# The first layer's second feed-forward sweep as seven block products, block sums formed in place, and the last sweep's residual work spread over ten tiles

## The chip, the cores and the metric

The kernel runs on one core of one Trainium2 chip. The metric is the device time of one execution in microseconds (us), taken as the median of several runs. Every number ahead of the prediction comes from the kernel before the change.

## The reference

Two layers of a diffusion backbone run over 1024 latent tokens and 256 context tokens, with 1024 features. The first layer mixes tokens with a convolution module, the second with attention. Each is followed by a feed-forward part, and that part is what the change touches:

```python
def swiglu(h, w1, w3, w2):
    return (jax.nn.silu(h @ w1) * (h @ w3)) @ w2
...
x = x + gf_x * rmsnorm(swiglu(fx, ffn_w1[i], ffn_w3[i], ffn_w2[i]), norm_g[i, 3])
```

All data are float32. The inner width of the feed-forward part is 2816, that is 22 tiles of 128.

## The kernel before

**Numbers as pairs.** Each float32 operand is split into a high part, rounded to the multiply format (`wh`), and a rest (`wl`). ACT casts the high part, DVE subtracts to get the rest (`split`, L158; `wload`, L137, for a weight just loaded). A product of two operands then takes three matmuls per block of 128 inner values: high by high, high by rest, rest by high (`mm3`, L166).

**Sweeps.** Activations lie with features on partitions and tokens along the free axis. The tokens are worked in three pieces: C (256 context tokens), L (the first 512 latent tokens) and R (the last 512). The function `ffn` (L790) makes one sweep over the 22 inner tiles. Layer one has two sweeps: the first for C and L, the second for R. Layer two has two as well: the first for L, the second for R. For each inner tile, `up` loads a 128x1024 tile of `w1` and one of `w3`, splits them, makes 48 matmuls of 512 columns, and forms the hidden tile. The 22 tiles form six groups of 4, 4, 4, 4, 3 and 3. After the first tile of the next group, `down` multiplies a group's hidden tiles by `w2` (96 matmuls of 512 columns for four tiles), and adds the result into the sweep's output (`evict`, L912, whose addition is L917). The last group is finished by `last` (L937).

**Block products.** In layer two's second sweep, all tiles but the first use `up_fast` (L844): `w1` and `w3` of that tile are taken as a 2x2 block matrix, the activations too (halves of the features by halves of the tokens), and the four block results come out of seven products in place of eight. Each product is 12 matmuls of 256 columns, 84 for a tile. The sums of activation blocks are formed once, by `forms` (L768). The sums of weight blocks are formed by DVE for each tile, into a tile of their own (`sums`, in the buffer KB), and then split. The weights come through three raw buffers (`self.raws`: two named `wr`, one named `q`), taken in turn by `raw` (L98). The split weights go to `wh` and `wl`, three buffers each, also in turn.

**Order.** Each engine runs its own list of instructions from first to last. The lists are made when the program is built, by a scheduler that looks at the dependencies, so an engine can have work of several tiles interleaved. Background work (residuals and norms of the pieces already done, and a first part of the attention's projections) is written as generators in a queue `bgq`. `pump` (L123) draws from it a share of each feed-forward step: 0.5 us of work per us of matmuls. In layer one's second sweep that background is `early` (L1351): the residuals of C and L (`final`, rows L692 and L695), the norm of C, the projections of C, and the norm of L (`apply`, rows L398, L403 and L404). In layer two's second sweep it is the residual of L.

Of the kernel before, what the change touches and what calls it, by code (L numbers as in the profile page):

```python
# [55 lines left out]
class Kern:  # L56
# [710 lines left out]

    def forms(self, x, tags, box):  # L768
# [18 lines left out]
        yield
        box += [(f[:, i, 0], f[:, i, 1]) for f in fs for i in range(2)]

    def ffn(self, l, fs, ytags, htags, boxes, tanh=False, parts=1, tail=None, fast=None):  # L790
# [53 lines left out]
        def up_fast(ft):  # L844

            n = ns[0] // 2
            xh, xl = fs[0][0]
            fm, sums = fast
            B11, B21, B22 = [lambda k, r=r, c=c: (xh[:, 4 * r + k, c * n:(c + 1) * n], xl[:, 4 * r + k, c * n:(c + 1) * n])
                             for r, c in ((0, 0), (1, 0), (1, 1))]  # L850
            T1, T2, T3, T4 = [lambda k, f=f: (f[0][:, k, :], f[1][:, k, :]) for f in fm]
            r1, r3 = self.raw(), self.raw()
            nc.sync.dma_start(r1, self.a["w1"][l, ft])
# [9 lines left out]
            def prod(out, w, x, first=True):  # L863
                for k in range(4):
                    (wh, wl), (bh, bl) = w(k), x(k)
                    nc.tensor.matmul(out, lhsT=wh, rhs=bh, start=first and k == 0, stop=False, skip_group_check=not first)  # L866
                    nc.tensor.matmul(out, lhsT=wh, rhs=bl, start=False, stop=False, skip_group_check=not first)  # L867
                    nc.tensor.matmul(out, lhsT=wl, rhs=bh, start=False, stop=k == 3, skip_group_check=not first)  # L868
            X = self.bank("sx")[:, :n]
            Y, Z = self.bank("sy")[:, :n], self.bank("mm")[:, :n]  # L870
            sa, h = self.sm(2 * n), self.sm(2 * n)
# [6 lines left out]
            nc.vector.tensor_tensor(s2, s1, a11, op=ALU.subtract)  # L878
# [4 lines left out]
            nc.scalar.copy(sa[:, n:], X)  # L883
            s3, s4 = sums[:, 1, :512], sums[:, 1, 512:]
            nc.vector.tensor_tensor(s3, a11, a21, op=ALU.subtract)
            nc.vector.tensor_tensor(s4, a12, s2, op=ALU.subtract)
# [4 lines left out]
            nc.vector.tensor_tensor(h[:, n:], h[:, n:], X, op=ALU.add)  # L891
            A22, = two(a22, 512)
            prod(X, A22, T4, False)
            nc.vector.tensor_tensor(sa[:, n:], sa[:, n:], Y, op=ALU.add)
            nc.scalar.activation(sa, sa, AF.Silu)
            nc.vector.tensor_tensor(h[:, n:], sa[:, n:], h[:, n:], op=ALU.mult)
            nc.vector.tensor_tensor(h[:, :n], sa[:, :n], X, op=ALU.mult)
            i = ft % (GRP + 1)
# [84 lines left out]
    def qk_pair(self, psE, psO, n, g, rope, wk, highs, sink, rq=None):  # L983
# [6 lines left out]
        self.qk += 1  # L990
        EO = wk[:, o:o + 2, :n]
        t12 = highs[self.qk % len(highs)][:, :, :n]
        E, O, t1, t2 = EO[:, 0], EO[:, 1], t12[:, 0], t12[:, 1]
# [40 lines left out]
    def qkv(self, h, col0, n, wk, rope=None, highs=()):  # L1034
# [3 lines left out]
        lat0 = col0 - CTX  # L1038
        highs = [wk[:, 6:8], *highs]
        if rope is not None:  # L1040
# [134 lines left out]
    def build(self):  # L1175
# [159 lines left out]
        self.bgq.append(rest_R())  # L1335
        for us in self.ffn(0, [(fv["C"][0], CTX), (fv["L"][0], 512)], (room[:, :2048].rearrange("p (k n) -> p k n", k=KT), "T5"), ("KB", "HS"),
                           (zv["C"], zv["L"])):
            self.pump(0.5 * us)
        self.drain()

# [8 lines left out]
        hC, hL, hR = [], [], []  # L1349

        def early():  # L1351
            yield from final(0, zv["C"][0], self.x1d, self.x2d, *PIECES["C"], 0, "KB")
            yield from final(0, zv["L"][0], self.x1d, self.x2d, *PIECES["L"], 0, "KB")
# [3 lines left out]
            wk = self.T("KB", [P, 8, 256])  # L1357
            yield from self.qkv(hC[0], 0, CTX, wk)
            self.xv = [self.cp.tile([P, 4], F32, tag=f"xv{i}", name=f"xv{i}") for i in range(2)]
            yield from self.norm_in(1, None, (None, "T3", "T2"), CTX, CTX + 512, hL, xt=zv["L"][0][0], keep=self.xv[0])  # L1360
# [27 lines left out]
    def attention(self, final, qr):  # L1388
# [102 lines left out]
        for i, us in enumerate(self.ffn(1, [(fL[0], 512)], ("T4",), ("HS",), (zL,), tanh=True)):  # L1491
            self.pump(0.95 * us)
            if i >= FT + 4 * (len(GROUPS) - 1) - 1:
                if fg is None:
                    self.drain()
                    fg = self.forms(yR[2], ("T6", "T3"), fm)
                next(fg, None)
# [3 lines left out]
        out = a["out"]  # L1501
        sums = self.T("KB", [P, 2, 1024])
        self.raws.append(self.room())
# [59 lines left out]
        for i, us in enumerate(self.ffn(1, [(fR[0], 512)], ("T1",), ("HS",), (zR,), parts=2, tail=(first, second),  # L1563
                                        fast=(fm, sums))):
            self.pump(0.5 * us)
            if i == FT + 4 * (len(GROUPS) - 1) - 1:
# [112 lines left out]
```

## Time and profile before

| What | Value |
|---|---|
| Median of 3 runs | 2950.51 us (2949.70 to 2955.74) |
| The profiled execution's own time | 2950.76 us |
| Its span, first to last instruction | 2949.0 us |
| Mean granted TensorE clock | 0.987 |
| Layer one's first sweep ends, second begins | at 1072.9 us of the span |
| Layer one's second sweep | 1072.9 to 1453.9 us |
| Layer two's second sweep up to `last` | 2578.9 to 2915.4 us |
| DVE busy over the span | 2034.8 us (69%) |
| ACT busy over the span | 1274.2 us (43%) |

The profile has one row for a group of instructions: the line of the kernel, the engine, the operation, the tile written and the tiles read (`wl<-wr,wh` writes `wl` from `wr` and `wh`; `ps` is the matmul result memory), how many, and the mean duration of one in ns. Behind the last bar stands how long the engine stood idle just before them, and which instruction ended the wait. PE is the matrix engine; DVE, ACT and POOL are the vector, scalar and GpSimd engines, and SP starts DMAs.

### The profile page before, as it was taken

The page shows a single profiled execution, that of the slowest core. Times are in us where ns is not written, and L with a number is a line of the kernel's source. Part 1 is how long each engine was busy: PE and PEld are TensorE (multiplying, and loading weights), DVE is VectorE, ACT ScalarE, POOL GpSimd, SP SyncE. Part 2 cuts the span into 40 slices and gives each one's busy share as a digit, 9 for nine tenths or more (in the row PEclk, how much of TensorE's full clock was granted, in tenths as well). Part 3 has the DMA queues.
Part 4 walks back from the last instruction along what each step waited for, and adds up shares of the span by engine and source line. Part 5 has one row for each costly group of instructions (what it writes and reads, how often), then busy time and mean ns, then how long its engine had stood idle before and what let it go on. Part 6 is the DMA issues. An engine that isn't in the chain of part 4 may idle for free.

```text
span 2949.0 us, 40809 instructions
## 1 busy us (share of the span) xinstructions
PE 2866.7 (97%) x15706; PEld 2424.9 (82%) x15706; DVE 2034.8 (69%) x3524; ACT 1274.2 (43%) x2118; POOL 223.2 (8%) x377
## 2 busy tenths in 40 slices
PE   8999989999999999999999999989999999999998
PEld 6888877888888888888878787767777778889997
DVE  6887887847556368433586899786666666776777
ACT  5222255432222134222345688645555543444444
POOL 0000001011122010000011111110000000010000
PEclk9999999999999999999999999999999999999999
DMA  6443434334355234332345211322222143343332
GB/s 248 132 126 98 122 126 149 128 126 131 110 175 187 65 115 150 107 97 89 129 161 164 88 46 45 102 81 81 70 69 83 60 136 97 123 167 94 101 99 88
DMA packets 131459, 336.46 MB, mean 114 GB/s; under 512 B 31297, under 2 KB 52833, under 8 KB 130113
## 3 DMA queue, kind: packets, MB, share of 16 engines
q1 hardware_dynamic: 77728, 222.33, 23.6%
q0 software_dynamic: 29344, 103.83, 10.9%
q10 hardware_dynamic: 24192, 7.70, 1.1%
q8 instruction: 123, 2.02, 0.3%
q14 instruction: 72, 0.58, 0.1%
HBM read 289.50 MB, written 38.93 MB: 111 GB/s over the span
## 4 chain that ended last, share of the span: by engine, by line
PE 88%; DVE 7%; DMA 2%; issue 2%; ACT 1%; POOL 0%; ACTq 0%; SPq 0%; DVEq 0%; POOLq 0%
PE ps L172 17%; PE ps L173 17%; PE ps L174 17%; PE ps L1100 4%; PE ps L1118 4%; PE ps L866 2%; PE ps L1124 2%; PE ps L868 2%; PE ps L453 2%; PE ps L867 2%; PE ps L454 2%; PE ps L1125 2%; PE ps L455 2%; PE ps L184 2%; PE ps L185 2%; PE ps L183 2%
## 5 line engine op out<-in xcount | busy, mean ns | idle before, releaser
L172 PE MATMUL ps<-T,wh 128*128 128x512 f32 (+1 forms) x1696 | 636.8, 376 | 0.6 <-DVE sm L830 0.4
L174 PE MATMUL ps<-T,wl 128*128 128x512 f32 (+1 forms) x1696 | 633.9, 374 | 3.0 <-DVE wl L148 3.0
L173 PE MATMUL ps<-T,wh 128*128 128x512 f32 (+1 forms) x1648 | 615.0, 373 | 0.1
L144 ACT CAST wh<-wr 128x1024 fp32r<-128x1024 f32 (+1 forms) x259 | 269.4, 1040 | 573.9 <-PE ps L173 416.3
L148 DVE TENSOR_TENSOR wl<-wr,wh 128x1024 fp32r<-128x1024 f32 (+1 forms) x259 | 313.0, 1209 | 225.0 <-ACT wh L144 222.2
L174 PEld LDWEIGHTS ps<-T,wl 128*128 128x128 f32 x1696 | 321.6, 190 | 58.0 <-DVE wl L148 3.6
L172 PEld LDWEIGHTS ps<-T,wh 128*128 128x128 f32 x1696 | 321.7, 190 | 56.1 <-ACT T L1463 1.7
L173 PEld LDWEIGHTS ps<-T,wh 128*128 128x128 f32 x1648 | 312.5, 190 | 52.4 <-DVE T L164 1.4
L1122 DVE TENSOR_TENSOR T<-ps,T 128x512 fp32r<-128x512 f32 x320 | 216.9, 687 | 108.4 <-ACT T L1121 107.6
L1121 ACT CAST T<-ps 128x512 fp32r<-128x512 f32 x320 | 186.1, 586 | 191.0 <-PE ps L1118 177.2
L173 PE MATMUL ps<-HS,wh 128*128 128x512 f32 x656 | 257.7, 393 | 0.0
L172 PE MATMUL ps<-HS,wh 128*128 128x512 f32 x608 | 238.4, 392 | 0.0
L174 PE MATMUL ps<-HS,wl 128*128 128x512 f32 x608 | 237.7, 391 | 0.0
L1118 PE MATMUL ps<-cst,T 128*128 128x128 f32 x1100 | 189.5, 275 | 3.1 <-DVE T L1122 3.1
L1106 DVE TENSOR_SCALAR_CACHE_REDUCE T<-ps,rq 128x1280 f32<-128x1280 f32 x110 | 170.1, 1546 | 28.0 <-PE ps L1100 22.1
L1118 PEld LDWEIGHTS ps<-cst,T 128*128 128x128 f32 x1100 | 132.8, 141 | 49.4 <-DVE T L1122 30.2
L866 PE MATMUL ps<-T,wh 128*128 128x256 f32 x588 | 167.2, 285 | 2.4 <-ACT wh L161 2.4
L868 PE MATMUL ps<-T,wl 128*128 128x256 f32 x588 | 165.4, 282 | 3.5 <-DVE wl L164 3.5
L1108 ACT ACTIVATE T<-T,mn 128x1280 f32<-128x1280 f32 x110 | 150.5, 1368 | 38.6 <-DVE T L1106 38.2
L867 PE MATMUL ps<-T,wh 128*128 128x256 f32 x588 | 165.2, 281 | 0.0
L917 DVE TENSOR_TENSOR T<-ps,T 128x512 f32<-128x512 f32 (+1 forms) x168 | 110.6, 662 | 77.7 <-PE ps L174 73.3
L1100 PE MATMUL ps<-KB,q 128*128 128x512 f32 (+1 forms) x576 | 145.2, 370 | 5.3 <-DVE HS L1106 3.1
(340 smaller groups left out, 5704.5 us busy)
## 6 DMA issues: line engine op xcount, KB each, us to landing
wr<-in_w SPq DMA_DIRECT2D x200, 512.0 KB, 3.5
q<-in_w SPq DMA_DIRECT2D x40, 512.0 KB, 3.5
wr<-in_pw SPq DMA_DIRECT2D x35, 512.0 KB, 3.6
HR<-in_wmodT POOLq DMA_DIRECT2D x56, 256.0 KB, 3.9
q<-in_wmodT POOLq DMA_DIRECT2D x56, 256.0 KB, 3.9
q<-qsd POOLq DMA_DIRECT2D x32, 256.0 KB, 3.3
wr<-in_wo SPq DMA_DIRECT2D x16, 512.0 KB, 3.6
qsd<-T POOLq DMA_DIRECT2D x14, 512.0 KB, 4.8
```

The lines of the kernel that those rows point to most:

```text
L144: nc.scalar.copy(hi, raw)
L148: nc.vector.tensor_tensor(lo, raw, hi.bitcast(F32), op=ALU.subtract)
L172: nc.tensor.matmul(out[:, :n], lhsT=wh, rhs=xh, start=k == 0, stop=False)
L173: nc.tensor.matmul(out[:, :n], lhsT=wh, rhs=xl, start=False, stop=False)
L174: nc.tensor.matmul(out[:, :n], lhsT=wl, rhs=xh, start=False, stop=k == nk - 1)
L866: nc.tensor.matmul(out, lhsT=wh, rhs=bh, start=first and k == 0, stop=False, skip_group_check=not first)
L867: nc.tensor.matmul(out, lhsT=wh, rhs=bl, start=False, stop=False, skip_group_check=not first)
L868: nc.tensor.matmul(out, lhsT=wl, rhs=bh, start=False, stop=k == 3, skip_group_check=not first)
L1100: nc.tensor.matmul(sc[:, k0:k0 + w], lhsT=q[:, h, :], rhs=kt[:, p * TOK + k0:p * TOK + k0 + w], start=p == 0, stop=p == 1)
L1118: nc.tensor.transpose(tp[:, h * P:(h + 1) * P], Ps[h][:, j * P:(j + 1) * P], c["ident"])
L1121: nc.scalar.copy(ph, tp)
L1122: nc.vector.tensor_tensor(pl, tp, ph.bitcast(F32), op=ALU.subtract)
```

## The change

The activation forms for layer one's second sweep are now made too: four DVE additions rebuild the float32 activations of R from their pairs (`both` in `forms`), then the forms are made as in layer two. Six of the eight steps are placed between the last steps of the first sweep, two behind the first tile of the second. The sums of weight blocks are written over the raw weights, one of them into a small buffer named `sb`, so that the weights are split in another order: the two top blocks, one sum alone (512 wide), a sum with a bottom block, and two sums. KB is then free. In layer two it gives two more raw buffers, five in all; in layer one there are three as before. Layer one's background takes 0.2 us per us up to the last group. The main part of the norm of L moves into a generator `late`, run beside `last` at 2.0. Layer two's share goes from 0.5 to 0.1.

```diff
+    def forms(self, x, homes, box, both=None):
...
+        if both is not None:
+            for b, k, c in ((b12, 0, 1), (b11, 0, 0), (b22, 4, 1), (b21, 4, 0)):
+                hi, lo = (v[:, k:k + 4, c * n:(c + 1) * n].bitcast(F32) for v in both)
+                nc.vector.tensor_tensor(b, hi, lo, op=ALU.add)
+                yield
...
             A11, A12 = two(r1)
             prod(X, A11, B11)
             prod(Z, A12, B21)
             nc.scalar.copy(sa[:, :n], X)
-            s1, s2 = sums[:, 0, :512], sums[:, 0, 512:]
-            nc.vector.tensor_tensor(s1, a21, a22, op=ALU.add)
-            nc.vector.tensor_tensor(s2, s1, a11, op=ALU.subtract)
-            S1, S2 = two(sums[:, 0])
+            tt(a11, a11, a21, ALU.subtract)
+            tt(s2, a22, a11, ALU.subtract)
+            S2, = two(s2, 512)
             prod(X, S2, T2, False)
-            nc.vector.tensor_tensor(sa[:, :n], sa[:, :n], Z, op=ALU.add)
+            tt(sa[:, :n], sa[:, :n], Z, ALU.add)
+            tt(a21, a21, a22, ALU.add)
+            S1, A22 = two(r3)
             prod(Y, S1, T1)
             nc.scalar.copy(sa[:, n:], X)
-            s3, s4 = sums[:, 1, :512], sums[:, 1, 512:]
-            nc.vector.tensor_tensor(s3, a11, a21, op=ALU.subtract)
-            nc.vector.tensor_tensor(s4, a12, s2, op=ALU.subtract)
-            S3, S4 = two(sums[:, 1])
+            tt(a12, a12, s2, ALU.subtract)
+            S3, S4 = two(r1)
             prod(X, S3, T3, False)
             nc.scalar.copy(h[:, n:], Y)
             prod(Y, S4, B22, False)
...
-            A22, = two(a22, 512)
             prod(X, A22, T4, False)
...
+            yield from self.qkv(hC[0], 0, CTX, None)
+            for _ in range(KT):
+                yield next(gl)
+
+        def late():
+            yield from gl
             self.wk = self.T("T5", [P, 8, 512])
+        gl = self.norm_in(1, None, (None, "T3", "T2"), CTX, CTX + 512, hL, xt=zv["L"][0][0], keep=xv[0])
         self.raws.append(self.room())
-        self.set_banks(mm=[0, 1, 2, 3], st=[5, 6], cv=[4, 7])
+        self.set_banks(mm=[0, 1, 2], sx=[3, 4], sy=[7], st=[5, 6])
         self.bgq.append(early())
-        for us in self.ffn(0, [(fv["R"][0], 512)], ("T1",), ("HS",), (zv["R"],)):
-            self.pump(0.5 * us)
+        for i, us in enumerate(self.ffn(0, [(fv["R"][0], 512)], ("T1",), ("HS",), (zv["R"],), fast=fm)):
...
+            if i == FT + 4 * (len(GROUPS) - 1) - 1:
+                self.drain()
+                self.bgq.append(late())
+                self.set_banks(mm=[0, 1, 2, 3], st=[5, 6], cv=[4, 7])
+            self.pump((0.2 if i < FT + 4 * (len(GROUPS) - 1) else 2.0) * us)
...
-        sums = self.T("KB", [P, 2, 1024])
+        more = self.T("KB", [P, 2, 1024])
+        self.raws += [more[:, 0], more[:, 1]]
         self.raws.append(self.room())
...
-            self.pump(0.5 * us)
+            self.pump(0.1 * us)
```

What this does to the order is shown at three places.

**First place: a plain tile of layer one's second sweep, on DVE and ACT** (the 17th tile, number 16; its raw buffers are `wr_73` for `w1` and `wr_74` for `w3`). Before, a tile of the same sweep was this on DVE (L836 is the hidden tile's multiplication, L148 the rest of a loaded weight, L164 the rest of the hidden tile, `HS`):

```order
L836 TENSOR_TENSOR sm<-sm,ps 128x512
L148 TENSOR_TENSOR wl<-wr_74,wh 128x1024
L164 TENSOR_TENSOR HS<-sm,HS 128x512
L148 TENSOR_TENSOR wl<-q,wh 128x1024
```

Now DVE has this (all of `up_fast`'s sums are recorded at L879, all of its splits at L164; `sb` is the small sum, `sm` the halves of the result):

```order
L879 TENSOR_TENSOR wr_73<-wr_73,wr_74 128x512
L879 TENSOR_TENSOR sm<-sm 128x256
L879 TENSOR_TENSOR sm<-sm,ps 128x256
L879 TENSOR_TENSOR sb<-wr_74,wr_73 128x512
L879 TENSOR_TENSOR wr_74<-wr_74 128x512
L164 TENSOR_TENSOR HS<-sm,HS 128x512
L164 TENSOR_TENSOR wl<-sb,wh 128x512
L879 TENSOR_TENSOR sm<-sm,ps 128x256
L164 TENSOR_TENSOR wl<-wr_74,wh 128x1024
L879 TENSOR_TENSOR wr_73<-wr_73,sb 128x512
L164 TENSOR_TENSOR wl<-wr_73,wh 128x1024
```

And ACT has this beside it (L885, L894 and L898 copy results out of `ps`: after the first, the third and the fourth product; L903 is the silu):

```order
L903 ACTIVATE sm<-sm 128x512
L161 CAST HS<-sm 128x512
L161 CAST wh<-sb 128x512
L885 COPY sm<-ps 128x256
L161 CAST wh<-wr_74 128x1024
L894 COPY sm<-ps 128x256
L161 CAST wh<-wr_73 128x1024
L898 COPY sm<-ps 128x256
```

The third row on DVE reads the last product of tile 15, and the sum `sb` for tile 16 now stands behind it; the sum into `wr_73`, whose split feeds the fifth product, stands behind the split of the two blocks in `wr_74`. On ACT the cast of that last pair stands behind the copy L894, which waits for the third product. Four tiles have the cast of `sb` ahead of the silu's hidden tile but the same last rows; the tile behind each `down` has all its casts ahead of L894.

**Second place: a plain tile of layer two's second sweep, on ACT.** Before (L875, L883 and L889 are the copies out of `ps`, L895 the silu):

```order
L875 COPY sm<-ps 128x256
L161 CAST HS<-sm 128x512
L161 CAST wh<-wr_73 128x512
L883 COPY sm<-ps 128x256
L161 CAST wh<-wr_74 128x1024
L889 COPY sm<-ps 128x256
L161 CAST wh<-KB 128x1024
L895 ACTIVATE sm<-sm 128x512
```

Now:

```order
L161 CAST wh<-sb 128x512
L903 ACTIVATE sm<-sm 128x512
L161 CAST wh<-KB 128x1024
L161 CAST HS<-sm 128x512
L885 COPY sm<-ps 128x256
L161 CAST wh<-wr_74 128x1024
L161 CAST wh<-KB 128x1024
L894 COPY sm<-ps 128x256
L898 COPY sm<-ps 128x256
```

The copy after the third product (L883 before, L894 now) moved behind two more 1024-wide casts: the tile's last pair and the next tile's first pair. In the first group of this sweep three tiles still have the last pair's cast behind it.

**Third place: the end of layer one's second sweep, on DVE, while `last` runs on PE.** Before (L917 adds a result from `ps` into the output, L390 sums squares, `q`, `wr_73` and `wr_74` are weights):

```order
L164 TENSOR_TENSOR HS<-sm,HS 128x512
L917 TENSOR_TENSOR T_8784<-ps,T_8784 128x512 x2
L390 TENSOR_TENSOR acc<-acc,sb 128x512
L917 TENSOR_TENSOR T_8784<-ps,T_8784 128x512
L148 TENSOR_TENSOR wl<-q,wh 128x1024
L390 TENSOR_TENSOR acc<-acc,sb 128x512
L917 TENSOR_TENSOR T_8784<-ps,T_8784 128x512
```

Now (L925 is the addition that was L917; L398 and L404 make the norm of L):

```order
L164 TENSOR_TENSOR HS<-sm,HS 128x512
L925 TENSOR_TENSOR T_8800<-ps,T_8800 128x512 x2
L148 TENSOR_TENSOR wl<-q,wh 128x1024
L390 TENSOR_TENSOR acc<-acc,sb 128x512
L398 SCALAR_TENSOR_TENSOR sb<-T_4324,col_7900,ps 128x512 x3
L404 SCALAR_TENSOR_TENSOR T_12381<-sb,mod_103,T_12380 128x512 x3
L398 SCALAR_TENSOR_TENSOR sb<-T_4324,col_7900,ps 128x512 x3
L404 SCALAR_TENSOR_TENSOR T_12381<-sb,mod_103,T_12380 128x512 x3
L925 TENSOR_TENSOR T_8800<-ps,T_8800 128x512 x2
```

Twelve instructions of the norm of L now stand between the second and the third addition of `last`'s results. `last` has eight results and four banks of `ps` for them.

More of the change, by code (lines that the diff above doesn't have):

```diff
@@ L847, in up_fast @@
             xh, xl = fs[0][0]
-            fm, sums = fast
             B11, B21, B22 = [lambda k, r=r, c=c: (xh[:, 4 * r + k, c * n:(c + 1) * n], xl[:, 4 * r + k, c * n:(c + 1) * n])
                              for r, c in ((0, 0), (1, 0), (1, 1))]
-            T1, T2, T3, T4 = [lambda k, f=f: (f[0][:, k, :], f[1][:, k, :]) for f in fm]
-            r1, r3 = self.raw(), self.raw()
+            T1, T2, T3, T4 = [lambda k, f=f: (f[0][:, k, :], f[1][:, k, :]) for f in fast]
+            r1, r3, s2 = self.raw(), self.raw(), self.sb(512)
             nc.sync.dma_start(r1, self.a["w1"][l, ft])
@@ L865, in prod, with tt @@
                     (wh, wl), (bh, bl) = w(k), x(k)
[L866 to L870, printed above, removed]
+                    skip = dict(skip_group_check=not first)
+                    nc.tensor.matmul(out, lhsT=wh, rhs=bh, start=first and k == 0, stop=False, **skip)
+                    nc.tensor.matmul(out, lhsT=wh, rhs=bl, start=False, stop=False, **skip)
+                    nc.tensor.matmul(out, lhsT=wl, rhs=bh, start=False, stop=k == 3, **skip)
+            def tt(o, u, v, op):
+                nc.vector.tensor_tensor(o, u, v, op=op)
+            X, Y, Z = self.bank("sx")[:, :n], self.bank("sy")[:, :n], self.bank("mm")[:, :n]
             sa, h = self.sm(2 * n), self.sm(2 * n)
@@ L990, in qk_pair @@
         self.qk += 1
-        EO = wk[:, o:o + 2, :n]
-        t12 = highs[self.qk % len(highs)][:, :, :n]
+        if wk is None:
+            EO, t12 = (self.sb(2 * n).rearrange("p (a n) -> p a n", a=2) for _ in range(2))
+        else:
+            EO, t12 = wk[:, o:o + 2, :n], highs[self.qk % len(highs)][:, :, :n]
         E, O, t1, t2 = EO[:, 0], EO[:, 1], t12[:, 0], t12[:, 1]
@@ L1038, in qkv @@
         lat0 = col0 - CTX
-        highs = [wk[:, 6:8], *highs]
+        highs = [] if wk is None else [wk[:, 6:8], *highs]
         if rope is not None:
@@ L1335, in build @@
         self.bgq.append(rest_R())
-        for us in self.ffn(0, [(fv["C"][0], CTX), (fv["L"][0], 512)], (room[:, :2048].rearrange("p (k n) -> p k n", k=KT), "T5"), ("KB", "HS"),
-                           (zv["C"], zv["L"])):
+        fm, fg = [], None
+        for i, us in enumerate(self.ffn(0, [(fv["C"][0], CTX), (fv["L"][0], 512)],
+                                        (room[:, :2048].rearrange("p (k n) -> p k n", k=KT), "T5"), ("KB", "HS"),
+                                        (zv["C"], zv["L"]))):
             self.pump(0.5 * us)
-        self.drain()
+            if i >= FT + 4 * (len(GROUPS) - 1) - 1:
+                if fg is None:
+                    self.drain()
+                    xh, xl = fv["R"][0]
+                    homes = self.pairs_in(self.T("T3", [P, 2, 2, 4, 256], F32R)) + [(xh[:, :4, 256:], xl[:, :4, 256:])]
+                    fg = self.forms(self.T("T2", [P, KT, 512]), homes, fm, (xh, xl))
+                    left = 6
+                elif i % 2 and left:
+                    left -= 1
+                    next(fg)
+        t = self.T("KB", [P, 2, 4, 256], F32R)
+        homes.append((t[:, 0], t[:, 1]))
         def final(l, y, src, dst, c0, c1, dcol, xtag, kind="st", eng=nc.gpsimd):
@@ L1349, in build @@
         hC, hL, hR = [], [], []
+        xv = self.xv = [self.cp.tile([P, 4], F32, tag=f"xv{i}", name=f"xv{i}") for i in range(2)]
         def early():
-            yield from final(0, zv["C"][0], self.x1d, self.x2d, *PIECES["C"], 0, "KB")
-            yield from final(0, zv["L"][0], self.x1d, self.x2d, *PIECES["L"], 0, "KB")
+            yield from final(0, zv["C"][0], self.x1d, self.x2d, *PIECES["C"], 0, "T2")
+            yield from final(0, zv["L"][0], self.x1d, self.x2d, *PIECES["L"], 0, "T2")
             yield from self.norm_in(1, None, (None, "T2", "T2"), 0, CTX, hC, xt=zv["C"][0][0])
@@ L1495, in attention @@
                     self.drain()
-                    fg = self.forms(yR[2], ("T6", "T3"), fm)
+                    homes = [p for t in ("T6", "T3") for p in self.pairs_in(self.T(t, [P, 2, 2, 4, 256], F32R))]
+                    fg = self.forms(yR[2], homes, fm)
                 next(fg, None)
```

33 lines of the change are left out of this document (17 added, 16 removed).

## The prediction

> **What bounds the kernel now.** I read the busy time of the engines first, then the chain of work that ended last, then the stages by windows.
>
> ```profile
> PE 2866.7 (97%) x15706; PEld 2424.9 (82%) x15706; DVE 2034.8 (69%) x3524; ACT 1274.2 (43%) x2118; POOL 223.2 (8%) x377
> PE 88%; DVE 7%; DMA 2%; issue 2%; ACT 1%; POOL 0%; ACTq 0%; SPq 0%; DVEq 0%; POOLq 0%
> ```
>
> The matrix engine is busy for 97% of the span and holds 88% of the chain. Fewer matmul microseconds are a gain only where ACT and DVE deliver the weights in time. The windows (length, then busy time and count of PE, PEld, DVE, ACT, POOL, then granted clock, DMA share and GB/s) show both sweeps that the change touches:
>
> ```profile
> 1035.00:1072.90 37.90, 37.90 (x214) 33.30 (x213) 20.68 (x36) 13.04 (x22) 2.88 (x4) 1.00 0.31 96
> 1072.90:1437.40 364.50, 364.14 (x1655) 299.98 (x1654) 182.99 (x294) 116.28 (x159) 14.24 (x24) 1.00 0.36 114
> 1300.30:1344.30 44.00, 44.00 (x194) 36.06 (x193) 14.36 (x15) 12.09 (x15) 0.00 (x0) 1.00 0.30 96
> 1437.40:1453.90 16.50, 16.50 (x73) 13.44 (x72) 13.02 (x18) 7.94 (x11) 2.88 (x4) 1.00 0.66 223
> 2578.90:2915.40 336.50, 330.60 (x2282) 307.52 (x2281) 248.48 (x381) 150.31 (x222) 7.39 (x12) 0.99 0.36 115
> 2600.00:2640.40 40.40, 34.50 (x269) 33.30 (x268) 35.50 (x58) 18.95 (x29) 7.39 (x12) 0.96 0.53 177
> 2662.20:2702.60 40.40, 40.40 (x338) 39.98 (x337) 30.36 (x47) 22.81 (x36) 0.00 (x0) 1.00 0.32 96
> ```
>
> Row 3 is four plain tiles of layer one's second sweep: 44.0 us, 11.0 a tile, 0.229 us a matmul, with DVE at a third. The last row is four block-product tiles of layer two: 40.4 us, 10.1 a tile, 1.44 us a product, with DVE at three quarters. The row above it is layer two's first group: same length, 5.9 us of it idle. Layer two's sweep should need 11.0 + 21 x 10.1 + 456 matmuls of the first five `down`s at 0.229 = 327.5 us; it took 336.5, so 9.0 us are lost, nearly all in that group.
>
> **The change part by part.** *Fewer matmuls.* In layer one 21 tiles go from 11.0 to 10.1 us: **-18.9 us** if PE never waits.
>
> *What the tiles must now wait for.* I walked the order of a tile with the durations below (busy time, mean ns), from the four block-product tiles, and with the lines of one engine in order of start (start, duration):
>
> ```profile
> L164 DVE TENSOR_TENSOR wl<-KB,wh 128x1024 fp32r<-128x1024 f32 x7 | 8.6, 1223 | 4.5 <-ACT wh L161 4.5
> L161 ACT CAST wh<-KB 128x1024 fp32r<-128x1024 f32 x7 | 7.3, 1046 | 7.0 <-issue 3.4 <-PE ps L173 1.9 <-PE ps L867 1.7
> L164 DVE TENSOR_TENSOR wl<-wr,wh 128x512 fp32r<-128x512 f32 x3 | 2.1, 687 | 0.0
> L161 ACT CAST HS<-sm 128x512 fp32r<-128x512 f32 x3 | 1.9, 623 | 0.0
> L883 ACT COPY sm<-ps 128x256 f32<-128x256 f32 x4 | 1.5, 374 | 3.5 <-PE ps L868 3.5
> L897 DVE TENSOR_TENSOR sm<-sm,ps 128x256 f32<-128x256 f32 x3 | 1.2, 415 | 0.0
> ```
> ```profile
> 2677.04 0.68 DVE L885 TENSOR_TENSOR KB<-wr,q 128x512 f32<-128x512 f32 x1
> 2677.64 0.68 DVE L878 TENSOR_TENSOR KB<-KB,wr 128x512 f32<-128x512 f32 x1
> 2678.36 0.69 DVE L886 TENSOR_TENSOR KB<-wr,KB 128x512 f32<-128x512 f32 x1
> 2679.08 1.22 DVE L164 TENSOR_TENSOR wl<-wr,wh 128x1024 fp32r<-128x1024 f32 x1
> 2680.23 0.41 DVE L891 TENSOR_TENSOR sm<-sm,ps 128x256 f32<-128x256 f32 x1
> ```
> ```profile
> 2678.00 1.05 ACT L161 CAST wh<-wr 128x1024 fp32r<-128x1024 f32 x1 [0.96 <-PE ps L867]
> ```
> ```profile
> 2676.34 0.28 PE L868 MATMUL ps<-T,wl 128*128 128x256 f32 x1
> 2676.46 0.28 PE L866 MATMUL ps<-T,wh 128*128 128x256 f32 x1
> ```
> ```profile
> 2676.66 0.37 ACT L883 COPY sm<-ps 128x256 f32<-128x256 f32 x1 [0.86 <-PE ps L868]
> ```
>
> Starts on DVE are 0.60 us apart for 512 columns (0.72 where the second needs the first), and 1.15 behind a 1024-wide rest. The cast ended at 2679.05 and its rest began 0.03 later. A product's last matmul at 2676.34 gives way to the next one at 2676.46, and the copy of its result starts 0.2 us behind that. Count from the start of a tile's first product; products end at 1.44, 2.89, 4.33, 5.77, 7.21, 8.66 and 10.1.
>
> The tile of the first place: the last product's multiplication runs at 0.2, `sb` is summed at 0.53, then the second sum at 1.13; ACT casts HS (0.65 to 1.27) and `sb` (to 1.89). DVE then makes the rest of HS (from 1.73), of `sb` (from 2.33, to 3.02; the third product wants it at 3.13, so no wait), the addition that reads the second product (3.09), the rest of `wr_74` (3.42 to 4.64, 0.1 late) and only then the sum into `wr_73` (4.56 to 5.25). ACT casts that to 6.30, DVE's rest ends at 7.53. The fifth product starts at 5.77 and its third matmul, the first to read the rest, wants it at 6.0: **a wait of 1.55 us**. Ten tiles of the sweep have this order (the four with the cast of `sb` first among them). Four tiles have a sum that is early, but the cast stands behind the copy that waits for the third product: copy at 4.53, cast from 4.81 to 5.86, rest to 7.1, wait **1.1 us**. The seven others have their casts ahead of the copy and are free, as the later groups of layer two were before. Sum: 10 x 1.55 + 4 x 1.1 = **+19.9 us**. This takes the gain of the seven products back. Bounds: nothing, if the copies' products end earlier than I take; twice that, if loads (below) come late as well. I take the walked value, since every row in it is of the same shape.
>
> *End of layer one's sweep, third place.* The twelve instructions of the norm of L:
>
> ```profile
> L398 DVE SCALAR_TENSOR_TENSOR sb<-T,col,ps 128x512 f32<-128x512 f32 x56 | 39.3, 744 | 5.5 <-PE ps L378 5.5
> L404 DVE SCALAR_TENSOR_TENSOR T<-sb,mod,T 128x512 fp32r<-128x512 f32 (+1 forms) x88 | 56.2, 675 | 4.0 <-ACT T L403 3.7
> ```
> ```profile
> 1441.18 1.39 DVE L917 TENSOR_TENSOR T<-ps,T 128x512 f32<-128x512 f32 x2 [0.82 <-PE ps L185]
> ...
> 1443.93 0.69 DVE L917 TENSOR_TENSOR T<-ps,T 128x512 f32<-128x512 f32 x1
> ```
>
> `last` begins at 1437.4 and makes a result each 16.5 / 8 = 2.06 us. With four banks, the seventh result, at 12.4, needs the third addition, which now begins after 5.2 (the two additions), 1.9 (a rest and a square sum) and 12 instructions about 0.65 apart (7.8), at 15 us, and ends at 15.7: **+3.3 us**, where before it ended at 7.2. Bounds 0 and 5: the nearer to the walked value.
>
> *The forms.* Four additions, four subtractions and four rests of 1024 columns, 12 x 1.2 = 14.4 us of DVE. Six of the eight steps lie in the end of the first sweep, where the first window row has DVE at 20.7 of 37.9 us: 17 us free. Cost nothing; without that cover some 2 to 5 us.
>
> *Layer two.* The 9.0 us went where the background residual, at 0.5 us per us, had DVE busy 35.5 of 40.4 us. It now takes 0.1, over ten tiles, and the sums no longer use a buffer that only one tile can hold: **-8.8 us**. Given back: three tiles of the first group with the late cast, 3 x 1.1 = **+3.3**, and, in some 14 later tiles, the copy after the third product now stands behind two casts of 1.05 us and ends 0.2 us behind the start of the product that writes its bank: **+2.8**. Bounds: -9 and +2.
>
> *Sum.* -18.9 + 19.9 + 3.3 - 8.8 + 3.3 + 2.8 = +1.6 us. The profiled execution took 2950.76 us (span 2949.0 and 1.76 around it), 0.25 over the median. Forecast **2952 us**, which is no change: 0.2% (5.9 us) is about what a measurement of this kernel can tell.
>
> **The rivals.** *Full gain.* Each tile's work fits in 10.1 us by sums (DVE 30.4 us in four tiles), and four tiles without a wait are in the row 2662.2. If PE's waits don't show, because casts that I have behind the copies run early, the terms 19.9, 3.3 and 2.8 fall away: 2950.8 - 18.9 - 8.8 + 3.3 = **2926 us**. Against it: engines follow their lists, and a list with the cast behind the copy can't run it earlier. *Half.* Latencies of 0.2 us and the early cast of some tiles halve the waits: 2952 - 13 = **2939 us**. For it: a wait in one tile moves all that ACT and DVE have ready for the next.
>
> *The loads become the bound (slower).* Layer one has three raw buffers. The one holding a tile's last pair comes free at 7.5 us, and the next tile's `w3` is loaded into it. Rows of issues (KB each, median us to landing), the first two and the last over the sweep:
>
> ```profile
> wr<-in_w SPq DMA_DIRECT2D x36, 512.0 KB, 3.5
> q<-in_w SPq DMA_DIRECT2D x19, 512.0 KB, 3.5
> KB<-x1d POOLq DMA_DIRECT2D x4, 512.0 KB, 5.6
> ```
>
> It lands at 11.1, half a microsecond before the next tile begins. That tile's sums, cast and rest of `sb` (0.7 + 0.7 + 0.6 + 0.7) are wanted at 3.13, so it must land by 12.0 on this scale: a load of more than 4.45 us starts to cost. At the 5.6 us of the third row each of 14 tiles loses 1.15: **+16, 2968 us**. The DMA share of 0.36 speaks against it, since with it the median is 3.5.
>
> *The clock (slower).* Waits can lower the granted clock:
>
> ```profile
> 2607.70:2611.10 3.40, 0.97 (x6) 0.77 (x6) 3.40 (x6) 1.00 (x2) 1.63 (x3) 1.00 0.40 154
> 2619.90:2623.30 3.40, 1.07 (x7) 0.66 (x6) 3.40 (x7) 2.52 (x3) 0.00 (x0) 1.00 0.17 31
> ```
> ```profile
> 2607.38 0.28 PE L867 MATMUL ps<-T,wh 128*128 128x256 f32 x1
> ...
> 2611.65 0.41 PE L866 MATMUL ps<-T,wh 128*128 128x256 f32 x1
> 2611.86 0.41 PE L867 MATMUL ps<-T,wh 128*128 128x256 f32 x1
> ```
>
> After 3.4 us with PE busy 0.97, matmuls start 0.21 apart in place of 0.12. The clock of 0.96 over 40.4 us is worth one such stretch of 3.4 us at half speed, so the second window, with 1.07, had no such follower. In a tile with a wait of 1.55 us, 3.4 us hold at least 1.85 us of work; from about 1.0 downwards it would trip. If it tripped in all 14 tiles, each would lose 3.4 / 2 = 1.7: **+24, 2976 us**. The Trainium skill ("TensorE: Matmul & The Clock Gate", section "A second HAM failure mode: psum-queue depth-cycling") says that frequent micro-idles between groups of matmuls can make the clock oscillate, without a whole idle window; that speaks against this change, and by it the time would be this rival's. The two windows above bear it out only where PE is idle for over two thirds of a stretch.
>
> **How the numbers follow.** Chances: the forecast 0.50 (2943 to 2961 by its bounds: nearly 0.40 within 0.2%, 0.05 to each side), half 0.18, full gain 0.14, loads 0.10, clock 0.08. So faster by over 0.2% 0.37, within 0.40, slower 0.23. The likeliest one's own range is 2943 to 2961. The range that leaves out the clock and the outer part of the full gain and of the loads, together under 0.2, is 2926 to 2966.
>
> **What would show it.** In the changed profile: four tiles of layer one's second sweep in a row should take 44 to 47 us in place of 40.4, with PE idle before the matmuls of line 876 (those that read `wl`), released by DVE's line 164, about 1.5 us in ten tiles and 1.1 in four. Windows of `last` should hold one PE wait of about 3 us, released by line 925. Layer two's first group should lose its idle 5.9 us and its clock read 1.00. The forecast is wrong if the four tiles take 40.4 (full gain), if the granted clock in the sweep is under 0.98 (clock), or if ACT's casts there wait for DMAs (loads).

## The result and the profile after

| | before | after |
|---|---|---|
| Median | 2950.51 us (2949.70 to 2955.74) | 2965.05 us (2961.65 to 2966.95) |
| Profiled execution, its span | 2950.76, 2949.0 us | 2966.95, 2965.2 us |
| Ratio | | 1.0045, 95% interval 1.003 to 1.006 |

The changed kernel is slower by 0.45%. That is inside the stated range (2926 to 2966) by 1 us, outside the range of the forecast itself (2943 to 2961), and on the side that had a chance of 0.23. The first answer is in the same windows of the profile of the changed kernel (length, busy time and count of PE, PEld, DVE, ACT, POOL, granted clock, DMA share, GB/s): layer one's second sweep, four block-product tiles of it in a row (with 12 short matmuls of the background and one of the next `down` between theirs), its `last`, layer two's second sweep, and four later tiles of that.

```profile
1072.90:1447.10 374.20, 356.98 (x2406) 325.83 (x2406) 287.73 (x492) 165.23 (x258) 16.86 (x28) 0.99 0.36 114
1306.20:1354.40 48.20, 45.22 (x350) 43.42 (x349) 34.38 (x64) 21.97 (x35) 0.00 (x0) 0.96 0.32 98
1447.10:1469.80 22.70, 18.14 (x72) 14.17 (x71) 21.13 (x32) 13.07 (x19) 3.07 (x5) 0.92 0.54 188
2599.80:2931.10 331.30, 329.54 (x2281) 305.96 (x2280) 252.29 (x381) 151.94 (x222) 7.37 (x12) 1.00 0.36 114
2677.90:2718.30 40.40, 40.40 (x338) 39.93 (x337) 32.89 (x49) 23.82 (x36) 0.00 (x0) 1.00 0.38 115
```

Layer one's sweep has 18.9 us less of matmuls and is 9.7 us longer (374.2 for 364.5). PE, idle there for 0.4 us before, now is for 17. Four tiles take 48.2 us, more than the 44.0 of the plain form, while four of the same kind in layer two take 40.4. `last` is 6.2 us longer (22.7 for 16.5). Layer two's sweep is 5.2 us shorter.

From here on a tile has its number in the sweep, counted from 0 for the plain one. What ended the waits is seen on DVE in tile 16 (start, duration, group, idle time before and what ended it), in the load that it waits for (KB, us to landing), on PE beside it, and on PE and DVE in `last`, one fence each:

```profile
1338.38 0.42 DVE L879 TENSOR_TENSOR sm<-sm,ps 128x256 f32<-128x256 f32 x1 [0.76 <-PE ps L876]
1340.64 0.69 DVE L879 TENSOR_TENSOR wr<-wr,wr 128x512 f32<-128x512 f32 x1 [1.85 <-DMA wr<-in_w]
```
```profile
wr<-in_w SPq DMA_DIRECT2D x1, 512.0 KB, 4.9
```
```profile
1343.66 0.39 PE L874 MATMUL ps<-T,wh 128*128 128x256 f32 x1 [1.20 <-ACT sm L885]
```
```profile
1464.00 0.50 PE L183 MATMUL ps<-HS,wh 128*128 128x512 f32 x1 [4.30 <-DVE T L925]
```
```profile
1455.33 2.06 DVE L398 SCALAR_TENSOR_TENSOR sb<-T,col,ps 128x512 f32<-128x512 f32 x3
1457.31 2.07 DVE L404 SCALAR_TENSOR_TENSOR T<-sb,mod,T 128x512 fp32r<-128x512 f32 x3
1459.30 2.06 DVE L398 SCALAR_TENSOR_TENSOR sb<-T,col,ps 128x512 f32<-128x512 f32 x3
1461.27 2.07 DVE L404 SCALAR_TENSOR_TENSOR T<-sb,mod,T 128x512 fp32r<-128x512 f32 x3
1463.26 1.28 DVE L925 TENSOR_TENSOR T<-ps,T 128x512 f32<-128x512 f32 x2
```

Tile 16 starts at 1339.59. Its first sum needs `w3`, which lands 1.0 us later: DVE idles 1.85 us for the load, and PE loses 4.0 us in that tile, 1.7 of them at half clock. The load is issued at 1335.61, when tile 15's last split has read its raw buffer, and takes 4.9 us. In `last`, the block of twelve instructions stands just where the order had it, and PE waits for the addition behind it.

Sum for the profiled executions, forecast in brackets. The sweep +9.7 (+1.0), `last` +6.2 (+3.3), layer two -5.2 (-2.7), the stages between the two layers' second sweeps about +5 (0). Most of the last seems not to be the kernel's, as the experiments on the middle suggest.

For them I use three lengths, read from the starts of matmuls on PE: from the last matmul of the first tile of layer one's second sweep to the last of the first projection of the latent piece L ("layer one", with `last`), from there to the last of the first tile of layer two's second sweep ("middle"), and from there to the first of its `last` ("layer two").

| Kernel | median us | ratio to before | layer one | middle | layer two |
|---|---|---|---|---|---|
| before | 2950.5 | 1 | 380.9 | 1125.3 | 325.5 |
| after | 2965.1 | 1.0045 | 396.4 | 1130.2 | 320.4 |
| layer two alone | 2947.5 | 0.9984 | 379.7 | 1127.5 | 320.4 |
| five raw buffers from tile 15 | 2954.3 | 1.0014 | 388.9 | 1126.1 | 320.4 |
| three raw buffers in layer two | 2991.7 | 1.0132 | 398.8 | 1129.0 | 341.0 |
| four raw buffers in layer two | 2966.0 | 1.0046 | 396.9 | 1128.9 | 320.4 |
| layer two's share 0.5 | 2973.4 | 1.0071 | 396.4 | 1127.4 | 328.8 |
| no background in layer one's sweep (one execution) | 2976.0 | | 407.5 | 1129.0 | 320.7 |
| late norm spread | 2959.8 | 1.0024 | 396.2 | 1124.9 | 320.4 |
| before with 9 matmuls more | 2955.6 | 1.0007 | 381.3 | 1127.6 | 325.5 |
| before with 15 matmuls more | 2955.3 | 1.0010 | 380.7 | 1127.7 | 325.5 |
| before with share 0.1 | 2942.6 | 0.9965 | 380.0 | 1126.1 | 317.0 |
| five raw buffers, late norm spread | 2941.4 | 0.9962 | 375.3 | 1125.8 | 320.4 |
| the same, layer two with own sums | 2937.5 | 0.9942 | 374.5 | 1124.8 | 317.1 |

Intervals stand with each run below; the kernel before was timed again with each set (medians 2951.5 to 2954.4).

### The profile page after: what moved, and what is told of

Read it like the earlier page. It is cut to its first block, busy times and chain, and to the rows that moved or that the text cites. A ratio compares the mean times of both kernels' runs of the same rounds, so it can differ in the third digit from the quotient of the medians.

```text
span 2965.2 us, 42721 instructions
## 1 busy us (share of the span) xinstructions
PE 2864.0 (97%) x16462; PEld 2452.4 (83%) x16462; DVE 2159.8 (73%) x3746; ACT 1331.8 (45%) x2227; POOL 222.5 (8%) x377
## 4 chain that ended last, share of the span: by engine, by line
PE 83%; DVE 9%; DMA 3%; ACT 2%; issue 2%; ACTq 0%; POOL 0%; SPq 0%; DVEq 0%; POOLq 0%
PE ps L172 15%; PE ps L173 15%; PE ps L174 15%; PE ps L1110 4%; PE ps L1128 4%; PE ps L874 3%; PE ps L876 3%; PE ps L875 3%; PE ps L453 2%; PE ps L1134 2%; PE ps L455 2%; PE ps L454 2%; PE ps L1135 2%; PE ps L184 1%; PE ps L185 1%
## 5 line engine op out<-in xcount | busy, mean ns | idle before, releaser
L174 PE MATMUL ps<-T,wl 128*128 128x512 f32 (+1 forms) x1360 | 502.1, 369 | 3.0 <-DVE wl L148 3.0
L172 PE MATMUL ps<-T,wh 128*128 128x512 f32 (+1 forms) x1360 | 503.9, 371 | 0.9 <-DVE sm L838 0.4
L173 PE MATMUL ps<-T,wh 128*128 128x512 f32 (+1 forms) x1312 | 483.5, 369 | 0.0
L144 ACT CAST wh<-wr 128x1024 fp32r<-128x1024 f32 (+1 forms) x225 | 233.3, 1037 | 434.7 <-PE ps L173 323.7
L148 DVE TENSOR_TENSOR wl<-wr,wh 128x1024 fp32r<-128x1024 f32 (+1 forms) x225 | 271.5, 1207 | 175.2 <-ACT wh L144 173.8
L874 PE MATMUL ps<-T,wh 128*128 128x256 f32 x1092 | 313.3, 288 | 13.0 <-ACT wh L161 8.3
L876 PE MATMUL ps<-T,wl 128*128 128x256 f32 x1092 | 305.6, 283 | 2.3 <-DVE wl L164 1.9
L875 PE MATMUL ps<-T,wh 128*128 128x256 f32 x1092 | 306.9, 281 | 0.0
L174 PEld LDWEIGHTS ps<-T,wl 128*128 128x128 f32 x1360 | 258.5, 190 | 43.7 <-DVE wl L148 3.3
L172 PEld LDWEIGHTS ps<-T,wh 128*128 128x128 f32 x1360 | 258.5, 190 | 43.2 <-ACT T L1498 1.7
L173 PEld LDWEIGHTS ps<-T,wh 128*128 128x128 f32 x1312 | 249.7, 190 | 38.1 <-DVE T L164 0.7
L874 PEld LDWEIGHTS ps<-T,wh 128*128 128x128 f32 x1092 | 206.6, 189 | 24.0 <-ACT wh L161 14.1
L876 PEld LDWEIGHTS ps<-T,wl 128*128 128x128 f32 x1092 | 205.8, 190 | 4.8 <-DVE wl L164 4.6
L875 PEld LDWEIGHTS ps<-T,wh 128*128 128x128 f32 x1092 | 207.3, 190 | 0.4
```

The source lines that it names most:

```text
L144: nc.scalar.copy(hi, raw)
L148: nc.vector.tensor_tensor(lo, raw, hi.bitcast(F32), op=ALU.subtract)
L172: nc.tensor.matmul(out[:, :n], lhsT=wh, rhs=xh, start=k == 0, stop=False)
L173: nc.tensor.matmul(out[:, :n], lhsT=wh, rhs=xl, start=False, stop=False)
L174: nc.tensor.matmul(out[:, :n], lhsT=wl, rhs=xh, start=False, stop=k == nk - 1)
```

## The experiments

**Layer two alone.** Everything in layer one (its `forms`, fast tiles, `late`) as before the change.

```diff
-        for i, us in enumerate(self.ffn(0, [(fv["R"][0], 512)], ("T1",), ("HS",), (zv["R"],), fast=fm)):
+        for us in self.ffn(0, [(fv["R"][0], 512)], ("T1",), ("HS",), (zv["R"],)):
...
```

> Layer one as before the change, layer two as after it. Layer two's second sweep took 336.5 us before (2578.9 to 2915.4) and 331.3 us after (2599.8 to 2931.1), 5.2 us less. If the parts are independent, the time is 2950.5 - 5 = 2945 us. If layer two's gain is only found behind the changed layer one (because its later start moves it against the stretches of half clock, one of which lay in it before and none after: 1.7 us), it is 2947 us.

0.9984 (0.9975 to 0.9992): 4 us faster, with the same 320.4 us in layer two as in the full change. So layer two's part gains, and layer one's part costs about 18 us. The time is the 2947 us expected for a gain that needs the changed layer one, but that theory fails: layer two has its whole gain here, and it is the middle that took 2.3 us more than in the profile of before.

**No background in layer one's sweep.** 0.2 becomes 0; one execution.

```diff
-            self.pump((0.2 if i < FT + 4 * (len(GROUPS) - 1) else 2.0) * us)
+            self.pump((0.0 if i < FT + 4 * (len(GROUPS) - 1) else 2.0) * us)
```

> As after the change, but layer one's second sweep draws no background; all of it comes ahead of the last stage, so the time as a whole rises by tens of us and only the tiles are read. Theory of the background: tiles 2 to 11, which were 1.1 to 2.5 us over 10.0 us, fall to the mean of the tiles that had none (12 to 21: 0 to 1.5 us, 0.6 without the one of 3.8). Theory of the cast's place or of the raw buffers: they wait as before, 1 us or more in at least half of them.

It took 2976.0 us, since all the background now comes ahead of the last stage. I take the times between the starts of a tile's successive matmuls and what they have over 10.02 us a tile (84 times 0.119), without the times of other work put between: the 21 tiles lost 25.9 us, against 25.8 with background. Four tiles in a row (13 to 16) took 46.3 us:

```profile
1287.80:1334.10 46.30, 42.92 (x339) 40.57 (x338) 32.96 (x50) 22.02 (x35) 0.00 (x0) 1.00 0.34 98
```

The background is not what the tiles wait for. The first tile behind each `down`, which lasts 16 to 22 us, waits for nothing again; the two or three behind it wait.

**Five raw buffers in layer one's last third.** From the tile at which the background is done, two more raw buffers are taken from T2, free there until the norm of L is written.

```diff
+                del self.raws[3:]
...
+            if not self.bgq and len(self.raws) == 3 and i < FT + 4 * (len(GROUPS) - 1) - 2:
+                t2 = self.T("T2", [P, 2, 1024])
+                self.raws += [t2[:, 0], t2[:, 1]]
```

> As after the change, but from the tile at which layer one's background is done (about the 15th) two more raw weight buffers are taken from the free tile T2. Theory of the raw buffers: sums formed in place hold a raw buffer until the last split, and with three of them the next tiles' weights come late; with five, the waits of tiles 15, 16, 18, 19 and 21 (1.5, 3.8, 1.2, 1.0 and 0.2 us over 10.0) fall under 0.3 us each, and the sweep is 6 to 7 us shorter, 1.7 of it the half-clock stretch at 1345 us. Theory of the cast's place in ACT's list: the waits stay at 1 us or more.

1.0014 (1.0005 to 1.0023), 11 us less than the full change; tiles 1 to 12 lose what they lost, except tile 4 (5.2 us for 3.1, 1.6 of them at half clock), and tiles 13 to 20 lose nothing (0.1 us or less each over 10.02). Four of them, 13 to 16:

```profile
1309.50:1349.70 40.20, 40.20 (x338) 39.80 (x337) 33.40 (x50) 23.27 (x35) 0.00 (x0) 1.00 0.38 114
```

DVE and ACT do about the same work as in the 48.2 us above (33.4 and 23.3 us busy, against 34.4 and 22.0), and PE is never idle.

**Three raw buffers in layer two**, the same test from the other side, and then **four**.

```diff
-        self.raws += [more[:, 0], more[:, 1]]
+        self.raws += [more[:, 0]]
```

(The run with three leaves this line out, and the one ahead of it.)

> As after the change, but layer two keeps three raw weight buffers in place of five. Theory of the raw buffers: the 17 tiles behind its first group, which now take 10.1 us each with no wait over 0.25 us, wait as the tiles without background of layer one do (0 to 1.5 us, mean 0.8), and the time rises by 10 to 17 us. Theory of the cast's place: the order of the lists without background is what matters, and the time rises by under 3 us.

> As after the change, but layer two has four raw weight buffers (with five 2965.1 us, with three 2991.7 us). Theory of the loop: with three, a tile's second load goes into the buffer that the tile ahead holds until its last split; with four it goes into one that is free a tile earlier, so four are as good as five: 2965 us, within 3. Theory that each buffer of lead counts alike: about half of the 26.6 us, 2978 us.

With three: 1.0132 (1.0116 to 1.0147), 26.6 us over the full change. Four tiles (5 to 8) and one matmul of the next `down`:

```profile
2684.20:2730.70 46.50, 42.89 (x339) 40.73 (x338) 32.26 (x49) 22.55 (x36) 0.00 (x0) 1.00 0.32 98
```

46.5 us for 40.4: 1.5 us a tile where no background runs. With four: 1.0046 (1.0032 to 1.006), as with five, and layer two again takes 320.4 us. So it isn't lead in general that counts. With three buffers a tile's `w3` is loaded into the buffer that the tile ahead holds until its last split; with four into one that came free earlier.

**Layer two's share at 0.5**, all else as after.

```diff
-            self.pump(0.1 * us)
+            self.pump(0.5 * us)
```

> As after the change, but layer two's background is drawn at 0.5 us per us as before, with five raw buffers and sums in place. If the lower share brought the gain in layer two's sweep (336.5 to 331.3 us), the sweep goes back to 335 us or more and the time rises by 4 us. If the buffers and sums in place brought it, the sweep stays within 1.5 us of 331.3.

1.0071 (1.0057 to 1.0085): 8 us over the full change, all of it in layer two (328.8 for 320.4), and in its profile 5.1 of the 8 are three stretches of half clock from 2624.5 us on. **The kernel before with share 0.1** has the same number changed alone, the other way:

> The kernel before with one number changed: layer two's background is drawn at 0.1 us per us in place of 0.5; three raw buffers, and sums in a buffer of their own, as before. Theory that the share alone brought layer two's gain: its sweep falls from 336.5 to 331 or 332 us and the time is that of layer two alone, 2947 us. Theory that sums in place and five buffers are needed for it: the sweep stays at 334 us or more and the time at 2950 us or more.

0.9965 (0.9953 to 0.9977): layer two takes 317.0 us, less than in the full change, with three raw buffers and sums in a buffer of their own. The whole of its second sweep, and the stretch in which its background now runs:

```profile
2578.00:2905.90 327.90, 327.90 (x2281) 305.71 (x2280) 247.80 (x381) 149.99 (x222) 7.37 (x12) 1.00 0.38 118
2598.00:2640.00 42.00, 42.00 (x317) 40.11 (x316) 41.25 (x69) 23.25 (x35) 3.84 (x7) 1.00 0.52 169
```

PE has no idle time in 327.9 us, though DVE is busy for 41.25 of 42 us. So one number brought more than the whole of layer two's gain; the sums in place gave 3.4 us of it back. The spread is smaller than the title's ten tiles: on DVE the residual's sixteen instructions (L692, L695) start within 38 us after the change and within 23 before it, which is about four tiles for two.

**Late norm spread.** 2.0 becomes 0.7, so the norm of L stands between the additions in single steps.

```diff
-            self.pump((0.2 if i < FT + 4 * (len(GROUPS) - 1) else 2.0) * us)
+            self.pump((0.2 if i < FT + 4 * (len(GROUPS) - 1) else 0.7) * us)
```

> As after the change, but the norm of L beside the last stage of layer one's second sweep is drawn at 0.7 us per us in place of 2.0, so its twelve instructions no longer stand in one block on DVE between the second and the third addition. If that block causes the wait of 4.5 us at 1464 us, the last stage falls from 22.7 us (16.5 before the change) to 17 or 18 us, with the half-clock stretch behind it (1.7 us) gone, and the time by 4 to 6 us, less what the later end of the norm costs the projections (0 to 2 us). If the stage is bound by DVE's sum of work (21 us of 23), it stays over 21 us.

1.0024 (1.0013 to 1.0036), 5.3 us less. The window from the start of `last` on shows PE idle 0.08 us where it had waited 4.3:

```profile
1451.50:1472.00 20.50, 20.42 (x91) 16.52 (x90) 19.51 (x30) 12.75 (x19) 2.68 (x5) 1.00 0.59 209
```

`last` takes 16.3 us; the projections behind wait 1.1 us for the norm. In this profile the row "layer one" hides the gain, since its tile 4 waited 4.5 us for a load, against 2.7 in the profile of after; the medians show it.

**The middle.** The profiled run of after lost 5 us more than that of before in stages that the change doesn't touch. The granted clock is halved there in stretches of 3.41 us or a multiple, 41.0 us in all after and 30.7 before, and the stretches lie on a grid. So I moved the kernel before against the grid by adding matmuls.

```diff
                     pbs.append(self.bank("mm"))
+                    if l == 0 and len(ns) == 1:
+                        self.mm3(pas[-1], cols(w1), x, 3, n)
                     self.mm3s((pas[-1], pbs[-1]), (cols(w1), cols(w3)), x, KT, n)
```

(With 15 matmuls, the 3 is a 5.)

> The kernel before, with 9 matmuls of 512 columns added at the start of layer one's second sweep (2.06 us of PE; they compute a part of a result that is then computed anew). The order of all other instructions is the same. Stretches of half clock lie on a grid of 3.413 us; the change moved the stages behind layer one by 15.9 us, that is 4 x 3.413 + 2.25. Theory of the grid: this shift of 2.06 us puts those stages in nearly the same place on the grid, and they lose about 5 us more, as behind the change: 2950.5 + 2.1 + 5 = 2957 to 2958 us. Otherwise 2952.6 us.

> As the run with 9 added matmuls, with 15 (3.43 us, one step of the grid). Theory of the grid: the stages behind lie as they did, and nothing else is lost: 2950.5 + 3.4 = 2954 us, so less than with 9. If added time in itself, or another cause, brings the loss, it is 2954 us or more and above the run with 9 by 1.4 us.

1.0007 (0.9999 to 1.0016) and 1.0010 (1.0001 to 1.0019), where the added matmuls alone are worth 1.0007 and 1.0012: no sign of the grid's place in the medians. The grid's own place against the start differs from execution to execution (the first half-speed stretch began between 60.5 and 63.7 us in the profiles). The middle took 1124.8 to 1130.2 us with no order among the kernels, so most of the 5 us looks like the draw of two single executions. Whether the changed kernel has a loss of 1 or 2 us there remains open.

**The parts put together.** Five raw buffers also in the first third, in the free end of HR, until the projections of C need it; five from T2 as above; the late norm at 0.7.

```diff
+            del self.raws[3:]
             self.vst = self.T("HR", [P, NKV, NJ, P], F32R)
...
+        self.raws += [room[:, 2048:3072], room[:, 3072:4096]]
...
```

> As after the change, with three things: layer one's second sweep has five raw weight buffers except while the background of its middle third runs (two in the free part of HR at first, two in T2 from the tile at which the background is done), and the norm of L beside the last stage is drawn at 0.7. The two parts tried alone gave -10.8 us (five buffers from the 15th tile) and -5.3 us. If the raw buffers also cause the waits of tiles 2 to 8 (10 us together over 10.0 us a tile), another 5 to 10 us go, and the time is 2939 to 2944 us, faster than the kernel before and than layer two alone (2947.5). If the background causes the waits there, the parts only add: 2949 us, no faster than before.

0.9962 (0.9949 to 0.9976), faster than the kernel before and than layer two alone. Tiles 4 to 7 now lose 0.1 us or less each, beside the background, and tile 8 0.35. Tiles 9 to 11, with three buffers, still lose 1.1 to 2.6 (1.7 of it at half clock), and tiles 2 and 3, which have five, 1.5 and 0.9; what those two wait for was not tested. So of the 25.8 us about 15 are shown to hang on the raw buffers (tiles 4 to 8 and 14 to 21).

**The same with layer two's own sums** (before's `up_fast` for layer two, share 0.1).

```diff
-                (up_fast if fast and ft else up)(ft)
+                ((up_own if isinstance(fast, tuple) else up_fast) if fast and ft else up)(ft)
...
```

> Layer one as in the run with five raw buffers and the late norm spread (0.9962 of the kernel before, 2941.4 us), layer two's sweep as before the change with sums in a buffer of their own, and background at 0.1 (alone 0.9965 of before). Layer two's changes alone gave 0.9984 of before, so the changed layer one is worth about 0.9978 and the two best halves together about 0.9943 of before, 2935 to 2937 us. If layer two is better by its own sums only in front of an unchanged layer one, it stays at 2941 us.

0.9942 (0.993 to 0.9954), 2937.5 us: the fastest that was run, 0.6% under the kernel before. The kernel before with share 0.1 has 0.9965, so that layer one's seven products, with the buffers, bring about 0.23%, some 7 of the 18.9 us that were hoped for.

## Why the prediction was right and wrong

**The seven products' gain is given back in the tiles: near in size, wrong in cause.** Forecast 19.9 us of waits over 10.1 us a tile; measured 24.1 on that scale (25.8 over 10.02), of which 3.4 is half clock in tiles 9 and 16. The number of free tiles is nearly right: eight lose 0.5 us or less (1, 5, 12, 13, 14, 17, 20 and 21), where seven were forecast, and four of the five tiles behind a `down` are among them. The place in the tile is not. The walk has no wait at the third product and all of it at the fifth, before the matmuls that read `wl`. Measured are 13.2 us at the third product and 2.2 at the fourth (the half clock is in these two) and 11.7 at the fifth, and PE idles mostly before the matmuls that read a cast, not a rest. Over the sweep:

```profile
L874 PE MATMUL ps<-T,wh 128*128 128x256 f32 x504 | 146.8, 293 | 11.7 <-ACT wh L161 7.1 <-ACT sm L885 3.8 <-ACT sm L898 0.3
L876 PE MATMUL ps<-T,wl 128*128 128x256 f32 x504 | 142.0, 286 | 2.3 <-DVE wl L164 1.9
```

I put the waits down to where casts stand on ACT, and weighed the loads apart as a rival, with half a microsecond to spare. The runs with five, four and three buffers show the shortage of raw buffers as the cause. A raw buffer is held until the last split (to 7.5 us by my walk, to 7.8 in tile 15), and only then is the next tile's `w3` loaded into it, so that this tile's sums, casts and rests must all be made inside the tile itself. In ten of the 21 tiles DVE idles for such a load before the tile's first sum (who waited for whom: us in total, times, longest):

```profile
DVE q L879 <- DMA wr<-in_w: 5.6, 4, 3.2
DVE wr L879 <- DMA wr<-in_w: 3.6, 4, 1.9
DVE wr L879 <- DMA q<-in_w: 1.2, 2, 1.0
```

With five buffers from tile 15 on in layer one, and with five or four in layer two behind its first group, no sum waits for a load any more; with three in layer two, eleven do. The order of the lists that I walked is built round the same shortage; with four or five buffers the program has another order and next to no wait. The step that failed is the split into a cast "behind the copy" and, apart from it, a load that "lands at 11.1, half a microsecond before the next tile begins": being that late is the wait, and it shows first at the third product. The rival's limit of 4.45 us for a load was passed twice by loads that DVE waited for: 4.9 us ahead of tile 16, and 6.4 us ahead of tile 4 (issued at 1114.89, landed at 1121.29), which lost 3.1 us. But tiles 6, 7, 11, 18 and 19 lost 1.2 to 1.4 us each behind loads of 3.4 to 3.6 us that DVE waited for, so the cost begins well below that limit. The first tile behind a `down` has had the `down` to be made ready in, the next a part of it (tiles 13 to 16 lost 0.05, 0.4, 1.6 and 4.0).

**The rest of the sweep: left out.** 28.6 us are lost in the sweep (18.9 + 9.7); 4.5 us lie outside the tiles' own matmuls, 3.1 of them at one place, where the projection of C has a chain of small instructions on DVE ahead of the tile's sums:

```profile
1230.12 0.17 DVE L1017 TENSOR_SCALAR nv<-ps 128x8 f32<-128x8 f32 x1 [3.92 <-PE ps L1014]
...
1232.54 0.29 DVE L1025 COPY sm<-nr 128x256 f32<-128x256 f32 x1
...
1233.97 0.68 DVE L879 TENSOR_TENSOR sb<-q,wr 128x512 f32<-128x512 f32 x1
```

Before, plain tiles had no sums to wait for on DVE. I costed the background at nothing beside the tiles; it isn't the cause of their waits, but here it adds one.

**The end of the sweep: right in mechanism, too small.** Forecast 3.3, measured 6.2: the wait itself 4.5, a half-speed stretch behind it 1.7. The spread norm removes it.

**Layer two: right in sign.** Recovered: the share alone gives 8.5 us (325.5 to 317.0; forecast 8.8). Given back: 3.4, in the first group (forecast 3.3), and there at the fifth product, as walked: four tiles lose 0.65 to 1.0 us each. The 2.8 for 14 later tiles, whose copy stands behind two casts, isn't there: four tiles take 40.4 us with PE never idle. That term was mis-sized; the measured value is 0.

**The clock: wrong threshold.** I took it to trip from about 1.0 us of PE in 3.4 downwards, and held waits of 1.5 us to be safe. It tripped three times in the sweep and `last` (5.1 us). Rows of the three stretches of 3.41 us ahead:

```profile
1232.39:1235.80 3.41, 0.88 (x4) 0.50 (x4) 3.03 (x7) 1.66 (x3) 0.73 (x2) 1.00 0.00 0
1341.62:1345.03 3.41, 1.91 (x14) 1.50 (x13) 3.41 (x8) 2.46 (x4) 0.00 (x0) 1.00 0.00 0
1461.08:1464.49 3.41, 0.49 (x2) 0.45 (x3) 3.41 (x7) 1.48 (x3) 0.00 (x0) 1.00 0.00 0
```

The middle one has PE busy 1.91 of 3.41, well over my threshold; the last section has a better measure. The stretch of the kernel before from which I took the threshold (2619.9 to 2623.3, 1.07 busy) doesn't lie on the grid: the nearest begin at 2617.97 and 2621.38, and the second of them has PE busy over 60%. The rival's price of 1.7 us each was right.

The forecast of 2952 us is 13 us short of the median. In the profiled run the missed terms are 4.2 us in the tiles, 4.5 in the rest of the sweep, 2.9 in `last` and about 5 in the middle, less 2.5 in layer two; in the medians the 5 is smaller. That the median is still inside the stated range is luck: the rest of the sweep and the middle had no term in it. The rival of the loads gave the nearest time, 2968 us, but it added its wait to the walked ones, and they are the same wait.

## What to carry to other kernels

Working in place saves a buffer and lengthens the hold of the one worked in: before it, count when each load's target comes free, over several tiles in a row, and ask whether one more buffer breaks the loop (here the fourth was worth 26 us and the fifth nothing). A stage that loses time to a background job may need only a smaller share of it: here one number, 0.5 to 0.1, brought 8.5 us, and the rebuilt sums beside it took 3.4 back. A change in several parts should be timed part by part, since here one part gained 4 us behind another that lost 18.

## What the runs showed of the hardware

The granted clock is decided in stretches of 3.413 us on a grid that starts at another place in every execution. PE's busy time alone does not tell when it is halved. In the kernel before, PE is busy for the whole of one stretch, and half clock follows; 24 of its 29 matmuls have a single column:

```profile
2484.85:2488.26 3.41, 3.41 (x29) 3.27 (x28) 1.24 (x4) 1.05 (x1) 0.00 (x0) 1.00 0.00 1
2488.26:2491.68 3.42, 3.42 (x10) 2.66 (x9) 3.01 (x16) 0.00 (x0) 0.00 (x0) 0.50 0.45 121
```
```profile
2485.05 1.84 PE L745 MATMUL ps<-cst,acc 128*128 128x1 f32 x16
2486.75 1.03 PE L745 MATMUL ps<-cst,HR 128*128 128x1 f32 x8
```

So I counted columns. At full clock 512 columns take 0.229 us; a stretch's share is the time that its matmuls' columns take at that rate. Over the profiles of all fourteen kernels, from 1050 us on, each stretch at full clock was taken with the stretch behind it. Below a share of 25%, all 82 were followed by half clock; from 25 to 40%, 51 of 76; above 40%, none of 7419. The stretch above has 21%. The three of the sweep and `last` have 10, 39 and 11%, and the stretches at 2617.97 and 2621.38 in the kernel before, which kept the full clock, 60 and 50%. An idle stretch isn't needed: waits that add up to some 60% of one can be enough, and they cost 1.7 us more. A wait of 1.5 us in a stretch leaves 56%, so a tile with one such wait does not halve the clock by itself. Which waits fall together in a stretch differs from execution to execution, and the five executions of the changed kernel spread over 5.3 us.
